# A hybrid decoder step: its first stage, channel tile by channel tile

## The chip, the cores and the metric

One core of one Trainium2 chip. The metric is the device time of one execution in microseconds (us); the kernel before takes 1694.86 us, the median of 3 runs (1690.61 to 1696.72). TensorE (PE) multiplies matrices, VectorE (DVE), ScalarE (ACT) and GpSimd (POOL) work element by element, and SyncE (SP) issues the DMA transfers.

## The reference

A prompt of 1024 tokens and a sample group of 8 x 4 = 32 tokens pass through two layers of width 1024: sliding-window attention, then gated DeltaNet. Every layer starts with a modulated norm and an input projection:

```python
def modulate(x, c, norm_g, w_mod, b_mod):
    shift, scale, gate = jnp.split(jax.nn.silu(c) @ w_mod + b_mod, 3, axis=-1)
    h = rms_norm(x, norm_g) * (1 + scale[:, None]) + shift[:, None]
    return h, gate[:, None]
...
    q, k, v, z = jnp.split(h @ w_in, [SWA_Q_W, SWA_Q_W + SWA_KV_W, SWA_Q_W + 2 * SWA_KV_W], axis=-1)
```

`c` is one row for the prompt and one for each of the 8 sample sequences, so nine rows in all. For a channel `d` and a token `t`, `h[t, d] = x[t, d] * rms[t] * Sc[d] + Sh[d]`, where `rms[t]` is 1 over the root of the mean square of the token's row, `Sc = norm_g * (1 + scale)` and `Sh = shift`.

## The kernel before, in words

All of it is float32. A projection takes its operands as a high and a low part (`hhi`, `hlo` for `h`; `wh`, `wl` for weights), each rounded so that PE can multiply it at full rate, and adds three products: high x high, low x high, high x low. The 1056 tokens stand in three groups of columns, 0 to 384, 384 to 768 and 768 to 1056; the 1024 channels are eight tiles of 128 partitions. One block of 128 output columns over all tokens and channels is therefore 8 x 3 x 3 = 72 matmuls.

The first stage makes `h` with channels on partitions and projects the first two blocks (keys of the first pair of heads, queries of the first group). Its steps:

- Loads, all issued by SP: nine tiles of rows of `x` (`xload`, eight of 128 rows and one of the 32 sample rows), the constants between the first and the second, then `w_mod` in two halves of eight tiles (`wmod_load`, 512 columns each of shift and scale), with the weights of the two blocks between them.
- `sq` (L625): ScalarE squares each row tile and sums it.
- `scale_x` (L631 to L639): DVE makes 1/rms of one to three row tiles by twelve small operations (`rsqrt`, L200 to L205) and multiplies the rows of `x` by it, ScalarE for three of the nine.
- `turn_x` (L650 to L659): PE transposes the scaled rows, eight squares of 128 x 128 for a tile, four to a bank of PSUM. ScalarE copies the first bank to `zo[0]`, DVE the second to `zo[1]`.
- `modulation_rows` (L311 to L322): silu of `c`, turned by PE into `cT`; the norm's weights and the bias, turned into `gT` and `bT`.
- `modulation` for one half of the channels: 16 matmuls (32 instructions, L344) into four strips of partitions, a copy `ma` by ScalarE (L354), and four matmuls with `fold64` (L360) that add the strips and turn them. `modulation_put` (L370 to L375) makes `Sh` and `Sc`.
- `shape_h(i)` for a half (L671 to L684): DVE (even tiles) or ScalarE (odd) makes `fu = zo * Sc + Sh` over the 1024 prompt columns, ScalarE rounds it to `hhi` (L674), DVE or GpSimd subtracts for `hlo` (L675). The 32 sample columns go by four GpSimd operations for four tiles together.
- `first_half(i, p_, kks)` (L702): the projection, half by half: first four channel tiles for the keys, the same four for the queries, then the other four for keys and for queries. The second half's modulation is interleaved by hand with the first tiles.

Around these steps a scheduler places the instructions of each engine; `issue_after` fixes some orders. Behind the stage come `kproj` and `qproj`, which empty the six banks (`khh`, `kll` at L823 to L826; `qs` at L889 and L890), the second query block (`project`, L567), the values (`vproj`, L1240) and then attention. From there on a planner (`Core`, whose wrapper is L89) writes down the order of each engine's instructions: it keeps a modelled time for every engine, counts each DMA at 0.45 us of issue and 2.4 us to landing, and lets pieces of work enter between projection matmuls when they are due. Weights of the projections are loaded by `load_raw` in pieces of 64 or 128 columns (L444), one projection ahead, and split by `split_w` (L456 on ScalarE, L457 on GpSimd). `keys_out` writes new keys and values, and copies the 124 kept rows of each sample cache from DRAM to DRAM.

Of the kernel before, what the change touches and what calls it, by code (L numbers as in the profile page):

```python
# [31 lines left out]
def constants():  # L32
# [35 lines left out]
    order = ["ident", "iu", "ones", "mku", "lo32", "bsel", "fold32", "fold64", "wmask", "hsel", "smask", "selp", "sels"]  # L68
# [151 lines left out]
def body(tc, I, O, cst_ap, dbg=None):  # L220
    nc = tc.nc
    from contextlib import ExitStack, nullcontext
    es = ExitStack()
# [29 lines left out]
    XB, FB, ZK, HK0, HK1 = 14, 3, 5, 7, 3  # L253
# [11 lines left out]
    gT = cp.tile([P, 2, KD], F32, name="gT")  # L265
    bT = cp.tile([P, 48], F32, name="bT")
# [9 lines left out]

    def xload(t):
        xt = xp.tile([P, D], F32, tag="xt", name="xt", bufs=XB)[0:P if t < NB else TS]
        nc.sync.dma_start(xt, xp_rows[t * P:(t + 1) * P] if t < NB else xs_rows)
        return xt  # L280

    def wmod_load(i):

        wms = []
        for k in range(KD):
            wt = xp.tile([P, D], F32, tag="xt", name="wm0", bufs=XB)
            nc.sync.dma_start(wt.rearrange("p (j c) -> p j c", j=2),
                              I["w_mod"][0, k * P:(k + 1) * P, 0:2 * D].rearrange("p (j c) -> p j c", j=2)[:, :, 512 * i:512 * i + 512])
            wms.append([wt[:, j * 512:(j + 1) * 512] for j in range(2)])
        return wms  # L290

    xts = [xload(0)]
    cst = cp.tile([P, nkeep], F32, name="cst")
    nc.sync.dma_start(cst, cst_ap[:, 0:nkeep])
    C = {k: cst[:, o:o + w] for k, (o, w) in COFF.items() if o < nkeep}
    ident = C["ident"]
    xts.append(xload(1))
    craw = xp.tile([P, D], F32, tag="fu", name="craw", bufs=FB)[0:9]
    nc.sync.dma_start(craw[0:1], I["c_prompt"])
    nc.sync.dma_start(craw[1:9], I["c_sample"])  # L300
    rows = xp.tile([64, P], F32, name="rows")
    nc.sync.dma_start(rows[0:16], I["norm_g"].rearrange("l (k p) -> (l k) p", p=P))
    nc.sync.dma_start(rows[16:64], I["b_mod"].rearrange("l (k p) -> (l k) p", p=P))
    xts += [xload(t) for t in range(2, NB + 1)]
    wm_half = [wmod_load(0)]

    x3 = None

    def modulation_rows():
        ce = xp.tile([P, D], F32, tag="fu", name="ce", bufs=FB)[0:9]  # L310
        nc.scalar.activation(ce, craw, AF.Tanh, scale=0.5)  # L311
        nc.gpsimd.tensor_scalar(ce, ce, 0.5, 0.5, ALU.mult, ALU.add)
        nc.gpsimd.tensor_tensor(ce, ce, craw, ALU.mult)
        nc.gpsimd.memset(cT, 0.0)
        pt = psb()
        for k in range(KD):
            nc.tensor.transpose(pt[:, k * 16:k * 16 + 9], ce[:, k * P:(k + 1) * P], ident[0:9, 0:9])
        nc.vector.tensor_copy(cT[:, :, 0:9], pt[:, 0:KD * 16].rearrange("p (k c) -> p k c", c=16)[:, :, 0:9])
        pt = psb()
        nc.tensor.transpose(pt[:, 0:64], rows, ident[0:64, 0:64])  # L320
        nc.vector.tensor_copy(gT.rearrange("p l k -> p (l k)"), pt[:, 0:16])
        nc.vector.tensor_copy(bT, pt[:, 16:64])  # L322

    Sh = [cp.tile([P, KD, 9], F32, name=f"Sh{l}") for l in range(2)]
# [3 lines left out]
    def modulation(l, load, js=(0, 1)):  # L328


        step, end = modulation_steps(l, load, js)
        for k in range(KD):
            step(k)
        return end

    def modulation_steps(l, load, js, pm=None):
        pm = pm or psb("mi")
        nj = len(js)

        def step(k):  # L340
            for q, wt in enumerate(load(k)):
                if nj == 1:
                    q += 2 * (k % 2)
                mm = nc.tensor.matmul(pm[32 * q:32 * q + 32, :], cT[:, k, :], wt,  # L344
                                      start=(k <= 2 - nj), stop=(k >= KD - 3 + nj), skip_group_check=True)
            return mm

        return step, lambda: modulation_end(l, js, pm)

    def modulation_end(l, js, pm):  # L350
        nj = len(js)
        w = 64 * nj
        ma = wp.tile([P, 512], F32, tag="wr", name="ma", bufs=4)
        nc.scalar.copy(ma, pm)  # L354
        mT = psb()
        for c in range(4):
            if nj == 2:
                mm = nc.tensor.transpose(mT[:, c * w:(c + 1) * w], ma[:, c * P:(c + 1) * P], ident)
            else:
                mm = nc.tensor.matmul(mT[:, c * w:(c + 1) * w], ma[:, c * P:(c + 1) * P], C["fold64"], start=True, stop=True)  # L360
        modulation_put(l, js, mT)
        return mm

    def modulation_put(l, js, mT):
        w = 64 * len(js)
        mv = mT[:, 0:4 * w].rearrange("p (c r) -> p c r", r=w)
        for q, j in enumerate(js):
            bs = bT[:, 24 * l + 4 * j:24 * l + 4 * j + 4]
# [254 lines left out]
    for t in range(NB + 1):  # L623
        parts = P if t < NB else TS
        sqs.append(nc.scalar.activation(sq[0:parts], xts[t], AF.Square, accum_out=xss[0:parts, t:t + 1]))  # L625
# [82 lines left out]
    for i, ts in enumerate(xb):  # L708
        last = nxt
        if i < 3:  # L710
            nxt = scale_x(xb[i + 1])
# [2014 lines left out]
```

## Time and profile before

| | us |
|---|---|
| median of 3 runs | 1694.86 |
| lowest, highest run | 1690.61, 1696.72 |
| span of the profiled execution | 1699.2 |
| PE busy in it | 1613.3 |
| DVE, ACT, POOL busy | 1207.9, 865.5, 581.8 |

The profile is of one execution, and its span, from the first to the last instruction, is the only time that it has; it is 4.3 us longer than the median of the runs. Times in it count from its first instruction. In a row of the timeline stand start, busy time, engine, line of the kernel, operation, what it writes and reads, shape, count, and in brackets how long the engine was idle before and what ended that. Rows merge neighbours of one kind: "x4" are four instructions. Matmul ends are modelled and overlap, so a pace is best read from one start to the next.

### The profile page before, as it was taken

The numbers are of one execution on the slowest core, as the hardware profiler recorded it, in microseconds if no ns is written. First come the engines' busy times: TensorE is split into PE (matmuls) and PEld (weight loads), VectorE is DVE, ScalarE is ACT, GpSimd is POOL, SyncE is SP. The second block draws the span as 40 slices with busy tenths as digits, with TensorE's granted clock in tenths as the row PEclk, the third lists the DMA queues.
The fourth block names the chain that finished last, engine by engine and source line by source line (L and its number), as shares of the span: only waits on it lengthen the run. The fifth ranks groups of instructions, "written<-read, shape, count | busy, mean of one in ns | idle before, by whom it ended". The sixth has DMA issues, their size and how long they took to land. (4 is left out here: it accounts for less than half of the span.)

```text
span 1699.2 us, 31431 instructions
## 1 busy us (share of the span) xinstructions
PE 1613.3 (95%) x10554; PEld 1417.4 (83%) x10554; DVE 1207.9 (71%) x3540; ACT 865.5 (51%) x2517; POOL 581.8 (34%) x1042
## 2 busy tenths in 40 slices
PE   6999999998999999999999999999999998989896
PEld 4988888986678899988989999899999996667784
DVE  5526676564665578878889788788788876367776
ACT  6625565443344565366463755655656654233332
POOL 2501111111222334363442644345344454333232
PEclk9999999998999999999999999999999999999998
DMA  9532121223343232132422324124241237855885
GB/s 345 158 123 73 53 59 48 59 81 93 116 136 105 79 77 65 59 99 73 118 56 69 89 66 129 46 79 111 54 124 49 55 97 225 245 165 169 243 259 166
DMA packets 281571, 191.76 MB, mean 113 GB/s; under 512 B 98361, under 2 KB 253881, under 8 KB 281378
## 3 DMA queue, kind: packets, MB, share of 16 engines
q1 hardware_dynamic: 281410, 189.75, 38.8%
q8 instruction: 84, 1.38, 0.4%
q14 instruction: 77, 0.63, 0.1%
HBM read 144.68 MB, written 47.04 MB: 113 GB/s over the span
## 5 line engine op out<-in xcount | busy, mean ns | idle before, releaser
L89 PE MATMUL ps_pj<-h2hi,wh 128*128 128x384 f32 (+1 forms) x1128 | 380.1, 337 | 0.0
L89 PE MATMUL ps_pj<-h2hi,wl 128*128 128x384 f32 (+1 forms) x1128 | 378.9, 336 | 0.6 <-POOL wl L89 0.5
L89 PE MATMUL ps_pj<-h2lo,wh 128*128 128x384 f32 (+1 forms) x1128 | 379.3, 336 | 0.0
L89 POOL TENSOR_TENSOR wl<-wr,wh 128x512 fp32r<-128x512 f32 x122 | 165.0, 1354 | 533.2 <-ACT wh L89 470.7
L89 PEld LDWEIGHTS ps_pj<-h2hi,wl 128*128 128x128 f32 x1128 | 213.5, 189 | 4.6 <-POOL wl L89 1.2
L89 PEld LDWEIGHTS ps_pj<-h2hi,wh 128*128 128x128 f32 x1128 | 213.5, 189 | 2.4
L89 PEld LDWEIGHTS ps_pj<-h2lo,wh 128*128 128x128 f32 x1128 | 213.2, 189 | 2.6
L89 POOL TENSOR_TENSOR xt<-xt,y 128x512 f32<-128x512 f32 (+1 forms) x48 | 63.6, 1329 | 174.3 <-DVE y L89 140.7
L89 PE MATMUL ps_pj<-hlo,wh 128*128 128x384 f32 (+1 forms) x360 | 119.6, 332 | 0.0
L89 PE MATMUL ps_pj<-hhi,wh 128*128 128x384 f32 (+1 forms) x360 | 119.0, 331 | 0.0
L89 PE MATMUL ps_pj<-hhi,wl 128*128 128x384 f32 (+1 forms) x360 | 118.7, 330 | 0.0
L89 DVE SCALAR_TENSOR_TENSOR vT<-XR,cT,vT 128x384 f32<-128x384 f32 (+1 forms) x144 | 91.8, 644 | 21.8 <-ACT vT L89 20.3
L89 DVE TENSOR_TENSOR X<-X,tmp 64x31 f32<-64x31 f32 (+15 forms) x248 | 94.5, 381 | 8.5
L89 DVE TENSOR_TENSOR tmp<-X 64x31 f32<-64x31 f32 (+15 forms) x248 | 95.9, 387 | 4.8 <-POOL X L89 1.5
L89 ACT CAST wh<-wr 128x512 fp32r<-128x512 f32 x122 | 75.1, 616 | 15.3 <-PE ps_pj L89 11.9
L89 PEld LDWEIGHTS ps_pj<-hlo,wh 128*128 128x128 f32 x360 | 68.2, 189 | 11.2 <-issue 11.1
L89 ACT COPY XR<-ps_pj 128x384 f32<-128x384 f32 (+1 forms) x96 | 43.2, 450 | 64.7 <-PE ps_pj L89 64.6
L89 PEld LDWEIGHTS ps_pj<-hhi,wh 128*128 128x128 f32 x360 | 68.3, 190 | 2.7 <-issue 2.7
L89 PEld LDWEIGHTS ps_pj<-hhi,wl 128*128 128x128 f32 x360 | 68.2, 189 | 2.1 <-issue 2.1
L89 ACT ACTIVATE prob<-prob,nm 128x256 f32<-128x256 f32 (+1 forms) x128 | 62.2, 489 | 14.9 <-DVE nm L89 14.7
L89 POOL TENSOR_TENSOR Xd<-Xc,cst 32x128 f32<-32x128 f32 x128 | 63.6, 497 | 16.1 <-DVE UZ L89 6.7
L89 ACT ACTIVATE qe<-ps_mi,Eg 128x128 f32<-128x128 f32 x112 | 35.0, 364 | 65.6 <-PE ps_mi L89 65.6
(575 smaller groups left out, 4177.2 us busy)
## 6 DMA issues: line engine op xcount, KB each, us to landing
wr<-in_gdn_w_in SPq DMA_DIRECT2D x96, 256.0 KB
S<-in_state_gdn_s SPq DMA_DIRECT2D x40, 256.0 KB
xt<-in_x_prompt SPq DMA_DIRECT2D x16, 512.0 KB
wm<-in_w_mod SPq DMA_DIRECT2D x16, 512.0 KB
wr<-in_swa_w_in SPq DMA_DIRECT2D x64, 128.0 KB
wmod<-in_w_mod SPq DMA_DIRECT2D x32, 256.0 KB
wm<-in_w_mod SPq DMA_DIRECT2D x32, 256.0 KB
DP<-gcr SPq DMA_DIRECT2D x64, 128.0 KB
```

Of the source, the lines that this page charges most:

```text
L89: inst = fn(*args, **kwargs)
```

## The change

The stage is written anew, channel tile by channel tile, and the planner's wrapper now stands around it, so that each compute engine follows the order of the program:

- The host lays out the inputs in other order (no arithmetic): `w_mod`'s shift and scale columns in eighths (`wm0`, one channel tile each, two loads of 512 KB with 4 KB for a partition), the nine rows of `c` with channels on partitions and norm weights and bias already turned (`cgb`), `swa_w_in` in blocks of 128 output columns (`winb`), the first two blocks' weights for two channel tiles at a time (`win01`), the values' weights (`winv`).
- SP's loads of the stage are held in one order (`queued`): x first, with only `ident` and `fold32` of the constants, then two eighths with the first weights, the other constants, and so on.
- Rows of `x` are turned as they are. DVE copies both banks of a tile. 1/rms is made in two parts, of five row tiles and of four, and spread over all partitions by nine small matmuls (`spread_x`) into `rsb`.
- For each channel tile: `modulate` (8 matmuls of 256 columns), `fold` (2 matmuls with `fold32`, two DVE operations for `Sc` and `Sh`), `shape_h` (DVE: `u = zo * Sc * rsb`; ScalarE: `hhi = u + Sh`; DVE: `hlo = u + Sh - hhi`; four small GpSimd operations for the sample columns), then both blocks' projections.
- In `keys_out`, the two cache copies are issued only after the write of the new values.

The core of the diff:

```diff
+    queue = []
+    def queued(dst, src):
+        inst = nc.sync.dma_start(dst, src).ins
+        if queue:
+            tc.add_manual_dep(inst, queue[-1], ...)
+        queue.append(inst.name)
...
+    def turn_x(n, t):
+        parts = P if t < NB else TS
+        for kk in range(2):
+            pt = psb(("pj3", "lg", "pj3", "lg", "pj3", "ob")[(2 * n + kk) % 6])
+            for j in range(4):
+                k = kk * 4 + j
+                nc.tensor.transpose(pt[:, j * parts:(j + 1) * parts], xts[t][:, k * P:(k + 1) * P],
+                                    ident[0:parts, 0:parts])
+            nc.vector.tensor_copy(zo[kk][:, :, t * P:t * P + parts],
+                                  pt[:, 0:4 * parts].rearrange("p (q t) -> p q t", q=4))
+        nc.scalar.activation(sq[0:parts], xts[t], AF.Square, accum_out=xss[0:parts, n:n + 1])
+
+    def scale_x(n0, n1):
+        sv = sm.tile([P, n1 - n0], F32, tag="sv4", name="sv4")
+        nc.vector.tensor_scalar(sv, xss[:, n0:n1], 1.0 / D, EPS, ALU.mult, ALU.add)
+        rsqrt(nc, sm, rsx[:, n0:n1], sv, n1 - n0, tag=f"rx{n0}")
+
+    def spread_x(gi):
+        a, b = GRP[gi]
+        pb = psb(("lg", "ob", "lg")[gi])
+        for t in range(3 * gi, 3 * gi + 3):
+            parts, n = P if t < NB else TS, turns_x.index(t)
+            nc.tensor.matmul(pb[:, t * P - a:t * P - a + parts], rsx[0:parts, n:n + 1].to_broadcast([parts, P]),
+                             ident[0:parts, 0:parts], start=True, stop=True)
+        nc.scalar.copy(rsb[:, a:b], pb[:, 0:b - a])
...
+    def modulate(e):
+        pm = psb("mi")[:, 0:256]
+        for k in range(KD):
+            q = k % 4
+            nc.tensor.matmul(pm[32 * q:32 * q + 32, :], cT[:, k, :], wms[e, k // 4][:, q, :], start=(k < 4), stop=(k >= 4),
+                             skip_group_check=True)
+        ma = xp.tile([P, 256], F32, tag="ma", name="ma", bufs=2)
+        nc.scalar.copy(ma, pm)
+        return ma
+
+    def fold(e, ma):
+        mT = psb("mi")
+        for c in range(2):
+            nc.tensor.matmul(mT[:, 32 * c:32 * c + 32], ma[:, c * P:(c + 1) * P], C["fold32"], start=True, stop=True)
+        nc.vector.tensor_scalar(Sc[0][:, e, :], mT[:, 32:41], bS[:, e:e + 1], gT[:, 0, e:e + 1], ALU.add, ALU.mult)
+        nc.vector.tensor_scalar(Sh[0][:, e, :], mT[:, 0:9], bT[:, e:e + 1], None, ALU.add)
+
+    def shape_h(k):
+        u = xp.tile([P, TP], F32, tag="fu", name="fu", bufs=FB)
+        sc, sh = Sc[0][:, k, 0:1], Sh[0][:, k, 0:1]
+        spans = [slice(0, GW), slice(GW, TP)]
+        for cs in spans:
+            nc.vector.scalar_tensor_tensor(u[:, cs], zo[k // 4][:, k % 4, cs], sc, rsb[:, cs], ALU.mult, ALU.mult)
+            nc.scalar.activation(hhi[:, k, cs], u[:, cs], AF.Identity, bias=sh)
+        for cs in spans:
+            nc.vector.scalar_tensor_tensor(hlo[:, k, cs], u[:, cs], sh, f(hhi[:, k, cs]), ALU.add, ALU.subtract)
...
+    def first_part(k, p_):
+        hi, lo = fws[k // 2]
+        for gi, (a, b) in enumerate(GRP):
+            for n, (x, y) in enumerate(((hi, hhi), (hi, hlo), (lo, hhi))):
+                nc.tensor.matmul(fps[p_][gi], x[:, 2 * p_ + k % 2, :], y[:, k, a:b], start=(k == 0 and n == 0),
+                                 stop=(k == KD - 1 and n == 2))
+
+    wmod_load(0)
+    first_load(0)
+    wmod_load(1)
+    for n, t in enumerate(turns_x):
+        turn_x(n, t)
+        if n == 1:
+            modulation_rows()
+        if n == 4:
+            scale_x(0, 5)
+    queued(cst[:, early:], cst_ap[:, early:nkeep])
+    wmod_load(2)
+    first_load(1)
+    spread_x(0)
+    scale_x(5, 9)
+    ma = modulate(0)
+    fws[0] = split_w(fraws.pop(0))
+    spread_x(1)
+    spread_x(2)
+    fold(0, ma)
+    shape_h(0)
+    ma = modulate(1)
+    wmod_load(3)
+    for k in range(KD):
+        if k + 1 < KD:
+            fold(k + 1, ma)
+            shape_h(k + 1)
+        first_part(k, 0)
+        if k % 2 == 0 and k + 2 < KD:
+            fws[k // 2 + 1] = split_w(fraws.pop(k // 2 + 1))
+        first_part(k, 1)
+        if k + 2 < KD:
+            ma = modulate(k + 2)
+        if k + 4 < KD:
+            wmod_load(k + 4)
+            if k % 2 == 0:
+                first_load(k // 2 + 2)
...
                 for new, old in ((nks, "cache_swa_k"), (nvs, "cache_swa_v")):
-                    nc.sync.dma_start(new[:, 0:P - DS, :], I[old][0].rearrange("b s h d -> b s (h d)")[:, DS:P, :])
+                    with tc.issue_after(values.ins):
+                        nc.sync.dma_start(new[:, 0:P - DS, :], I[old][0].rearrange("b s h d -> b s (h d)")[:, DS:P, :])
...
-        plan = [(win, {"k": lambda b: [(0, 1024 + b * P, P)], "q": lambda b: qpieces(b // 4, b % 4), "z": zpieces}[a](b))
-                for a, b in ORDER]
+        plan = [(winb[{"k": 0, "q": 2, "z": 10}[a] + b], [(0, 0, P)]) for a, b in ORDER]
```

The row tiles are turned in the order 0, 1, sample rows, 2 to 7 (`turns_x`).

285 lines of the change are left out of this document (88 added, 197 removed).

## The prediction

> **What bounds the kernel now.** I read the page first, then the stages in time, then the first 68 us engine by engine. The page:
>
> ```profile
> span 1699.2 us, 31431 instructions
> PE 1613.3 (95%) x10554; PEld 1417.4 (83%) x10554; DVE 1207.9 (71%) x3540; ACT 865.5 (51%) x2517; POOL 581.8 (34%) x1042
> ```
>
> TensorE (PE) is busy for 95% of the span. The table of stages says where it is not:
>
> ```profile
> 0.00:67.00 67.00, 50.40 (x304) 39.75 (x305) 38.29 (x92) 41.09 (x63) 28.76 (x28) 1.00 0.79 261
> 67.00:110.00 43.00, 42.40 (x322) 38.95 (x320) 9.98 (x27) 14.80 (x43) 7.62 (x6) 1.00 0.51 154
> ```
>
> After the name of a stage and its length stand the busy times of PE, weight loads, VectorE (DVE), ScalarE (ACT) and GpSimd (POOL), then the clock, the DMA share and GB/s. The first 67 us, which are all that the change rewrites, have 16.6 us of idle PE; the 43 us behind them have 0.6. Whatever the first stage saves or loses therefore passes on to a PE that is full. In order of time on PE:
>
> ```profile
> 16.14 1.11 PE L650 MATMUL ps_pj<-cst,xt 128*128 128x128 f32 x4 [3.96 <-DVE xt L639]
> 23.84 1.06 PE L650 MATMUL ps_pj<-cst,xt 128*128 128x128 f32 x4
> 24.69 1.06 PE L650 MATMUL ps_lg<-cst,xt 128*128 128x128 f32 x4
> ...
> 32.40 2.78 PE L344 MATMUL ps_mi<-wm,cT 128*32 128x512 f32 x24
> 35.95 1.10 PE L360 MATMUL ps_mi<-cst,ma 128*128 128x64 f32 x8 [0.76 <-ACT ma L354]
> 36.98 2.77 PE L344 MATMUL ps_mi<-wm,cT 128*32 128x512 f32 x20
> 39.68 0.44 PE L702 MATMUL ps_pj<-hhi,wh 128*128 128x384 f32 x1
> ...
> 49.82 0.33 PE L702 MATMUL ps_lg<-hhi,wh 128*128 128x384 f32 x1
> ...
> 55.63 0.33 PE L702 MATMUL ps_pj<-hhi,wh 128*128 128x384 f32 x1
> ...
> 67.26 0.33 PE L567 MATMUL ps_pj<-hhi,wh 128*128 128x384 f32 x1
> ```
>
> The transposes wait for rows that DVE has to scale first; the modulation waits for its weights; the projection (L702) starts at 39.7 and has ended at 67.26, where the next projection (L567) starts. From 49.82 to 55.63 it does four channel tiles for one block of weights: 5.81/4 = 1.45 us, so a channel tile for both blocks is 2.9 us and all eight are 23.2. The remaining 4.3 of the 27.6 us are the rest of the second modulation, its fold and short waits.
>
> **The change, part by part.** The new stage is a chain up to the first projection matmul, S, and then a loop up to the end E. I work out both and compare E with 67.26.
>
> *Loads.* Their amount is the same, their order is x first, then w_mod in eighths. ScalarE and the DMA view (GB/s in 40 slices of the first 60 us) give the arrivals:
>
> ```profile
> 4.61 1.28 ACT L625 ACT_TABLE_LOAD   x1 [4.61 <-DMA xt<-in_x_prompt]
> 7.31 1.06 ACT L625 ACTIVATE sq<-xt 128x1024 f32<-128x1024 f32 x1 [0.25 <-DMA xt<-in_x_prompt]
> GB/s 0 145 400 380 310 412 412 407 415 300 276 388 388 385 386 388 386 341 264 359 388 382 378 384 385 387 308 166 322 91 379 24 105 149 0 0 0 0 0 0
> ```
>
> x0 lands at 4.6. Between it and x1 come 836 KB now and 592 KB then, so x1 lands at 6.5; at some 386 GB/s each further 512 KB takes 1.36 us, the small pieces 0.5: x7 at 15.2, w_mod's first eighth (1 MB) at 17.9, the second, behind weights, at 21.3, the last at about 40. The loop below wants the last one at about 54, so the loads bound nothing; the new layout as such is costed at nothing, with 14 us of cover.
>
> *Rows and 1/rms.* Each row tile is eight transposes. Their pitch is 24.69 - 23.84 = 0.85 for four, 1.7 for a tile, slower than it arrives. They start at about 5.1 (ident), the 32 sample rows take 0.8, and x7 is through at 5.1 + 8 x 1.7 + 0.8 = 19.5. All copies out of PSUM now fall to DVE (ScalarE did half), with two chains for 1/rms between them:
>
> ```profile
> 7.09 0.15 DVE L631 TENSOR_SCALAR sv<-xss 128x1 f32<-128x1 f32 x1 [7.09 <-ACT sq L625]
> 9.40 0.75 DVE L639 TENSOR_SCALAR xt<-xt,rs 128x1024 f32<-128x1024 f32 x1
> ...
> 26.89 1.28 DVE L659 COPY zo<-ps_lg 128x512 f32<-128x512 f32 x2
> ```
>
> A chain is 9.40 - 7.09 = 2.3 us, a copy 0.6. Program order puts the first chain behind the fifth tile: 13.5 + 2.3 = 15.8, then four tiles at 1.2 reach 20.6, and the second chain 22.9. The scaling of the rows goes (0.75 or 1.15 a tile), and with it PE's waits; late next is this second chain. 1/rms is then spread over partitions by nine small matmuls, two instructions each at the transposes' 0.21: six of the nine follow the chain, 2.2 us cold, 1.1 at full clock. The squares, tanh, and the shorter modulation rows run beside arrivals; without that cover they would cost their 1.2 us a tile on ScalarE.
>
> *To the first matmul.* Needed are rows for fold, ScalarE's copy, shaping and GpSimd:
>
> ```profile
> 35.31 0.58 ACT L354 COPY ma<-ps_mi 128x512 f32<-128x512 f32 x1 [1.75 <-PE ps_mi L344]
> 37.65 1.24 ACT L673 ACTIVATE fu<-zo,Sh,Sc 128x1024 f32<-128x1024 f32 x1 [1.76 <-DVE Sc L375]
> 83.35 0.37 ACT L1245 COPY vsb<-ps_pj 128x256 f32<-128x256 f32 x1 [0.50 <-PE ps_pj L1240]
> 37.09 0.20 DVE L370 TENSOR_TENSOR Sh<-ps_mi,bT 128x36 f32<-128x36 f32 x1 [4.29 <-PE ps_mi L360]
> 39.59 1.54 DVE L675 TENSOR_TENSOR hlo<-fu,hhi 128x512 fp32r<-128x512 f32 x2
> 41.85 2.61 DVE L675 TENSOR_TENSOR hlo<-fu,hhi 128x1024 fp32r<-128x1024 f32 x1 [0.72 <-ACT hhi L674]
> L89 DVE SCALAR_TENSOR_TENSOR zo<-th,zo 128x384 f32<-128x384 f32 x16 | 9.1, 570 | 0.6
> 40.95 2.44 POOL L675 TENSOR_TENSOR hlo<-fu,hhi 128x1024 fp32r<-128x1024 f32 x1 [0.96 <-ACT hhi L674]
> L89 POOL TENSOR_TENSOR us<-us,tp 128x32 f32<-128x32 f32 x96 | 30.2, 314 | 8.0
> ```
>
> A fold is now four instructions, half of L360's eight: 0.5. Two DVE operations, 0.5 with the handover. The new three-operand product is not in the trace with 640 columns: at least 0.57 (its 384), at most 1.6 (2.61 x 640/1024, beside GpSimd); I take 0.85, nearest to 0.77 for 512. So 1.4 for both halves, 0.95 for ScalarE on the second half. Behind that on ScalarE's queue stands the copy of the next eighth, 0.37 + 0.1, and PE's fold of that eighth (0.5) is queued ahead of the first projection matmul. Sum: 0.5 + 0.5 + 1.4 + 0.95 + 0.5 + 0.5 = 4.4. S = 22.9 + 2.2 + 4.4 = 29.5, or 28.4 at full clock; I take 29.3. That is 10.4 us earlier than 39.7.
>
> *The loop.* What stood ahead of the projection now stands inside it. Per channel tile PE does 2.9 us of projection, then modulates an eighth, waits for ScalarE, folds. An eighth is 16 instructions of 256 columns; 24 of 512 took 2.78, so 0.058 each, 0.93, with the tail 1.03 (bounds 0.85, and 1.86 if a short one cost as much as a long one). The wait was 0.76 with a copy of 0.58; with 0.37 it is 0.56, and nothing covers it, since PE's order holds the projection behind the fold. So 1.03 + 0.56 + 0.5 = 2.1 us, six times after S: 12.5. E = 29.3 + 23.2 + 12.5 = 65.0.
>
> DVE per tile has 0.4 + 2 x (0.57 + 0.85) = 3.2 us; from the end of one fold to the last hlo it is 3.8 with ScalarE between, against a period of 5.0 plus 0.5 until that hlo is read. GpSimd's four small sample operations (0.3 to 0.8 each) and every second tile a weight split slow it: the 1024 column subtraction took 2.61, not twice 0.77, beside GpSimd's 2.44. I add 0.5 us over the loop (0 to 7).
>
> *Hand-over.* Before, the keys' banks were complete at 61.4 (55.63 + 5.8), 5.8 us ahead of the queries' last matmul; now both end together. The first key bank is complete 2.4 us before E, but the next projection needs it empty:
>
> ```profile
> 63.55 0.54 DVE L825 TENSOR_TENSOR kll<-ps_pj,khh 64x384 fp32r<-64x384 f32 x1
> 64.11 0.55 DVE L826 TENSOR_TENSOR kll<-ps_pj,khh 64x384 fp32r<-64x384 f32 x1
> 62.08 0.47 ACT L823 CAST khh<-ps_pj 64x384 fp32r<-64x384 f32 x1
> ```
>
> 0.57 for the first cast and four subtractions at 0.57 are 2.9 us: PE waits 0.5, with handovers 0.7. The next banks follow behind 4.2 us of matmuls each. Later projections only load in larger pieces; SP issues half as many, and PE waited for no weights there: 0.
>
> *Moved copies.* Two 992 KB cache copies leave SP's queue at 40.4 and 86.5 us for behind the values, some 20 us later than the second; next weights and modulation weights queue behind them:
>
> ```profile
> 40.44 0.86 SPq L89 DMA_DIRECT2D out_new_k_s<-in_cache_swa_k  x1
> 86.52 0.74 SPq L89 DMA_DIRECT2D out_new_v_s<-in_cache_swa_v  x1
> 110.00:200.00 90.00, 87.77 (x598) 74.71 (x596) 57.26 (x223) 51.90 (x177) 11.86 (x9) 1.00 0.29 84
> ```
>
> 1.6 us of issue, 2.6 us of transfer each at 386 GB/s, in a stage where DMA is 29% busy and weights are asked for one projection (12.6 us) ahead: 0, at most 5.
>
> **Sum.** 65.0 + 0.5 + 0.7 = 66.2 against 67.26: 1.1 us less, 1698.1 on the profiled execution's 1699.2. The median of the runs is 1694.86, 4.3 below that span, so 1693.8. A start 10 us earlier is nearly all given back inside the loop.
>
> **Rivals.**
>
> *A. The projection begins at half clock.* This clock exists here:
>
> ```profile
> 411.00:414.00 3.00, 0.98 (x24) 0.88 (x24) 1.98 (x10) 1.14 (x2) 0.00 (x0) 0.86 0.18 49
> 414.00:417.00 3.00, 2.44 (x3) 1.17 (x4) 0.09 (x1) 0.36 (x1) 0.00 (x0) 0.50 0.69 224
> 417.00:420.00 3.00, 3.00 (x7) 1.85 (x6) 0.52 (x1) 1.88 (x5) 0.00 (x0) 0.50 0.03 5
> 26.54 1.49 PE L344 MATMUL ps_mi<-wm,cT 128*32 128x512 f32 x2
> 30.61 0.60 PE L650 MATMUL ps_lg<-cst,xt 128*128 128x128 f32 x4
> ```
>
> After a thin stretch the granted clock was 0.50, and dense work needed some 5.3 us (414.6 to 419.9) to get it back. The transposes too took 1.06 for four before 26.5 us and 0.60 at 30.6, though the clock column shows 1.00 there. In the old stage modulations stood between transposes and projection; in the new one PE has only spreads, two eighths and two folds in the last 10 us before S, with idle gaps of up to 2.3. If S falls into half clock, 5.3 us do 2.65 us of work: 1693.8 + 2.7 = 1696.5. The Trainium skill, "TensorE: Matmul & The Clock Gate", section "Part 4: PE-mode transpose", says that transposes do not count as busy for the clock; by that rule the rows of transposes warm nothing, and this rival would be likely. Our trace agrees so far: the transposes ahead of 26.5 stayed at their long pace, and quicker ones are seen 4 us after the first modulation matmul. Against it: spreads and eighths are real matmuls, on PE for 6 to 8 of the 10 us before S, a longer run than those 4. 20%.
>
> *B. VectorE sets the loop (slower).* If GpSimd's operations meet DVE's in every tile, 2 x 1024 columns at 2.61 are 5.2, with folds and handover 6.2 us. It decides from 5.5 on. 0.7 us a tile over eight tiles (the first delays S), and 1 more at the hand-over: 1693.8 + 6.6 = 1700.4, slower than before. For it: the 2.61 row. Against: GpSimd has 1.6 us of sample work a tile, and 1.3 for a split every second, not 5. 17%.
>
> *C. All terms at their low ends.* Warm from the spreads on (S 28.4), 0.93 + 0.5 + 0.42 in the loop (11.1), hand-over hidden: E = 62.7, 4.6 less: 1690.3. 16%.
>
> *D. The planned stages shift.* The planner counts every DMA that is issued, and half of the weights' DMAs are gone; an order that comes out otherwise, or the moved copies, could move the waits of those stages. Price up to 8 us, either way: 1686 or 1702. 9%.
>
> *E. The change's order isn't reached*, since loads wait: at half the rate the last eighth lands at 65, 11 us late, which gives 1705; 14 us of slack speak against it; 2%.
>
> **Numbers.** Forecast 36%, the rest as given; its own range is 1691 to 1696. A to C and most of D lie between 1686 and 1702, which with 3 us between runs of one kernel is the range. Within 0.5% (8.5 us, about what a measurement of this kernel can tell from no change) lie the forecast and nearly all of A, B and C. Faster by more than that: D's lucky half and the low edge of C, 10%; slower: B's far end, D and E, 12%; within: 78%.
>
> **What would show it.** First L702-like matmul at 28 to 31, not 39.7; transposes still at 0.85 for four; DVE's second chain ending near 23; PE waiting some 0.56 for "ma" in each of six tiles and nothing like that for hlo; one wait below 1 us after the last first-stage matmul; the next projection at 65 to 67. An hlo wait in each tile would show B, clock below 1 around 30 us A. Wrong would be the whole sum if the transposes keep up with the arrivals (S by 3 us earlier), or if PE's idle time after 110 us changes by several us.

## The result, and the profile after

The changed kernel takes 1704.05 us (median of 6 runs, 1702.11 to 1707.83) against 1694.51 us (6 runs, 1690.61 to 1698.17) of the kernel before on the same chip: a ratio of 1.0055, 95% interval 1.0037 to 1.0073, or 9.5 us more. It is slower, just beyond the 0.5% that a measurement can tell from no change; the forecast was 1.1 us faster. Chips and executions differ by several us here: the execution of before that the prediction read, with its span of 1699.2, took longer than any of these six runs, and on other chips the median of before was 1699.5 to 1701.2. So ratios below are always against before on the same chip.

The page of the changed kernel, its first lines, and its two stages:

```profile
span 1700.9 us, 31581 instructions
PE 1620.1 (95%) x10643; PEld 1428.9 (84%) x10643; DVE 1214.1 (71%) x3546; ACT 859.2 (51%) x2516; POOL 581.8 (34%) x1065
```

```profile
0.00:67.00 67.00, 53.41 (x377) 44.83 (x378) 40.72 (x90) 29.63 (x52) 24.03 (x49) 0.92 0.60 230
67.00:110.00 43.00, 40.30 (x283) 36.79 (x282) 13.35 (x27) 19.08 (x51) 10.36 (x8) 0.92 0.50 167
```

The first row gained 3 us of busy PE and still isn't done at 67; the second, which had 0.6 us of idle PE, now has 2.7, and both have a granted clock of 0.92. PE's timeline says where:

```profile
14.46 0.60 PE L89 MATMUL ps_pj<-cst,xt 128*128 128x128 f32 x4
24.23 0.93 PE L89 MATMUL ps_ob<-cst,rsx 128*128 128x128 f32 x4 [2.80 <-DVE rsx L89]
30.72 1.06 PE L89 MATMUL ps_mi<-cst,ma 128*128 128x32 f32 x4 [1.29 <-ACT ma L89]
31.59 0.67 PE L89 MATMUL ps_pj<-hhi,wh 128*128 128x384 f32 x1
37.74 0.63 PE L89 MATMUL ps_mi<-cst,ma 128*128 128x32 f32 x4 [0.55 <-ACT ma L89]
42.92 0.63 PE L89 MATMUL ps_mi<-cst,ma 128*128 128x32 f32 x4 [0.55 <-ACT ma L89]
...
73.03 0.66 PE L542 MATMUL ps_pj<-hhi,wh 128*128 128x384 f32 x1 [2.66 <-DVE kll L803]
```

The spreads wait 2.80 us for the second 1/rms; the first projection matmul, S, stands at 31.59; from one fold to the next a tile takes 7.02 us the first time (30.72 to 37.74) and 5.18 after that; the next projection (L542) starts at 73.03, after a wait of 2.66 for the keys' bank, where L567 started at 67.26. The clock by stage (PEclk is the third number from the end of a row):

```profile
24.00:26.00 2.00, 1.77 (x9) 1.55 (x9) 0.16 (x1) 0.48 (x1) 0.00 (x0) 0.64 1.04 416
26.00:34.00 8.00, 6.71 (x35) 5.24 (x35) 5.48 (x11) 3.05 (x6) 4.32 (x10) 0.50 1.03 407
34.00:36.00 2.00, 2.00 (x12) 1.96 (x10) 1.05 (x2) 1.01 (x2) 1.19 (x2) 0.80 1.02 397
36.00:68.00 32.00, 28.68 (x235) 23.49 (x234) 19.39 (x36) 12.99 (x23) 15.26 (x28) 1.00 0.17 61
68.00:73.00 5.00, 2.37 (x14) 2.13 (x15) 3.57 (x8) 4.84 (x11) 2.25 (x2) 0.94 0.52 158
73.00:80.00 7.00, 6.97 (x24) 7.00 (x25) 5.36 (x11) 5.45 (x14) 5.00 (x4) 0.56 0.94 336
```

Both pauses, 2.80 and 2.66 us, are followed by half clock, once for about 10 us and once for 7. In the second stretch PE is full, so (1 - 0.56) x 7 = 3.1 us are lost outright. That is this execution; in the second trace of the same program (e5) half clock behind the hand-over ends after 3.4 us, and 1.6 are lost.

To place all versions on one scale I use one instruction that occurs once, far behind the first stage: ScalarE's copy of the second key pair's last columns. In before and after:

```profile
237.76 0.29 ACT L89 COPY kx<-ps_pj 128x160 f32<-128x160 f32 x1 [1.00 <-DVE kll L89]
```

```profile
243.28 0.29 ACT L89 COPY kx<-ps_pj 128x160 f32<-128x160 f32 x1 [1.00 <-DVE kll L89]
```

### The profile page after: what moved, and what is told of

Its sections match the earlier page's. It is cut to its first block, busy times and chain, and to the rows that moved or that the text cites. A ratio compares the mean times of both kernels' runs of the same rounds, so it can differ in the third digit from the quotient of the medians.

```text
span 1700.9 us, 31581 instructions
## 1 busy us (share of the span) xinstructions
PE 1620.1 (95%) x10643; PEld 1428.9 (84%) x10643; DVE 1214.1 (71%) x3546; ACT 859.2 (51%) x2516; POOL 581.8 (34%) x1065
## 5 line engine op out<-in xcount | busy, mean ns | idle before, releaser
L89 POOL TENSOR_TENSOR wl<-wr,wh 128x512 fp32r<-128x512 f32 x128 | 175.9, 1376 | 546.1 <-ACT wh L89 469.4
L89 PE MATMUL ps_pj<-hlo,wh 128*128 128x384 f32 (+1 forms) x376 | 125.0, 332 | 0.0
L89 PE MATMUL ps_pj<-hhi,wh 128*128 128x384 f32 (+1 forms) x376 | 124.7, 332 | 0.0
L89 PE MATMUL ps_pj<-hhi,wl 128*128 128x384 f32 (+1 forms) x376 | 123.8, 329 | 0.0
L89 ACT CAST wh<-wr 128x512 fp32r<-128x512 f32 x128 | 78.6, 616 | 15.2 <-PE ps_pj L89 12.3
L89 PEld LDWEIGHTS ps_pj<-hlo,wh 128*128 128x128 f32 x376 | 71.0, 189 | 11.5 <-issue 11.1
```

What stands on the lines that cost most here:

```text
L89: inst = fn(*args, **kwargs)
```

## The experiments

Theory 1: the loss is made in the first stage and at its hand-over (half clock around S, PE's wait for the keys' bank, half clock behind that). Theory 2: the later weights in blocks, the moved cache copies or the planner's order cost it. Rivals to single points stand with the runs. All versions, by next projection, marker (as above) and ratio to before on the same chip:

| run | next projection | marker | ratio, 95% interval |
|---|---|---|---|
| before; again (e9) | 67.26; 65.99 | 237.76; 236.56 | 1; 0.9997 (0.9979 to 1.0014) |
| after; again (e5) | 73.03; 73.82 | 243.28; 242.72 | 1.0055 (1.0037 to 1.0073); 1.0039 (1.0022 to 1.0056) |
| e1, e13 later only | 67.90; 66.81 | 236.27; 236.72 | 1.0016 (1.0001 to 1.0032); 1.0006 (0.9991 to 1.0020) |
| e11 copies only | 69.60 | 237.98 | 1.0006 (0.9986 to 1.0025) |
| e10, e14 first only | 75.53; 73.32 | 246.17; 243.97 | 1.0069 (1.0048 to 1.0090); 1.0052 (1.0035 to 1.0070) |
| e2 keys last | 70.69 | 244.00 | 1.0045 (1.0028 to 1.0062) |
| e3 idle matmuls | 71.42 | 240.40 | 1.0042 (1.0025 to 1.0059) |
| e4 lag 2 | 75.16 | 244.14 | 1.0043 (1.0027 to 1.0059) |
| e6 bank order | 72.97 | 242.21 | 1.0037 (1.0020 to 1.0054) |
| e7 lag 1 and bank order | 72.75 | 240.61 | 1.0028 (1.0013 to 1.0043) |
| e12 copy hidden | 70.47 | 239.44 | 1.0031 (1.0018 to 1.0044) |
| e8 all repairs | 67.76 | 235.61 | 1.0009 (0.9992 to 1.0026) |
| e15 order | 69.09 | 239.20 | 1.0012 (0.9998 to 1.0026) |
| e16 order, no idle matmuls | 66.82 | 236.24 | 0.9998 (0.9985 to 1.0011) |
| e17 banks | 63.36 | 232.86 | 0.9968 (0.9953 to 0.9983) |

An interval is some 5 us wide, so single ratios tell the ends of the table apart and not its neighbours; the traces tell the rest. They have a scatter of their own. Up to the end of VectorE's second chain for 1/rms the programs after, e4 to e7, e10, e12 and e14 do the same work, and yet that chain ends between 23.00 us (e6) and 25.63 (e10): with the landing of x's second row tile, for which PE waits up to 1.56 us (e10), and with the moment at which the transposes come to full pace (between 8.5 us in e6 and 16.2 in e12). This moves next projection and marker alike.

**Which part of the change: e1, e13, e11, e10, e14, e9, e5.** In the first two only the later parts are put into before:

```diff
-        plan = [(win, {"k": lambda b: [(0, 1024 + b * P, P)], "q": lambda b: qpieces(b // 4, b % 4), "z": zpieces}[a](b))
-                for a, b in ORDER]
+        plan = [(winb[{"k": 0, "q": 2, "z": 10}[a] + b], [(0, 0, P)]) for a, b in ORDER]
...
-                    nc.sync.dma_start(new[:, 0:P - DS, :], I[old][0].rearrange("b s h d -> b s (h d)")[:, DS:P, :])
+                    with tc.issue_after(values.ins):
+                        nc.sync.dma_start(new[:, 0:P - DS, :], I[old][0].rearrange("b s h d -> b s (h d)")[:, DS:P, :])
```

e11 has the second edit alone; e10 and e14 undo both in the changed kernel; e9 and e5 are before and after themselves, once more.

> The kernel before, with its whole first stage kept; only the weights of the later projections come in blocks and the two cache copies are moved behind the values. Theory 1 (the loss is made in the first stage and at its hand-over): ratio 1.000 to the kernel before, within 0.0015, and the planned stages stand where they stood. Theory 2 (the later weights, the moved copies or the planner's order cost the part that the first 75 us do not show, some 4 us): ratio 1.0025.

> The kernel of the first experiment once more (before, with the later weights in blocks and the copies moved). If blocks or copies cost 2 to 3 us: ratio 1.0016 again, and both together exclude 1.000. If that was chance: ratio 1.000 within 0.0015.

> The kernel before with only the two cache copies moved behind the values; weights as they were. Theory 1: ratio 1.000 within 0.0015. Theory 2 (the copies, now in the queue ahead of the second projection's weights, delay a load that PE waits for): ratio 1.0015, with a wait of PE between 90 and 130 us that the kernel before hasn't.

> The changed kernel with its first stage, but the later projections' weights taken from the old array in pieces and the two cache copies issued where they were: the complement of the first experiment. Theory 1 (all of the loss is made in the first 75 us): ratio as the changed kernel's, 1.0045 within 0.0015, next projection at 73 us. Theory 2 (the blocks and the moved copies cost 2 to 3 us of it): ratio 1.003.

> The kernel with only the new first stage once more. Its first trace had the next projection at 75.5 us, 2.5 later than the changed kernel's, with the same instructions in the first stage. If that was the execution's own scatter in the time at which the transposes come to full clock: next projection at 73 to 74.5, ratio 1.0045 to 1.006. If the pieces of the later weights cost it: 75.5 again, ratio 1.007.

> The kernel before itself once more, as a measure of what two executions of one program differ by. Ratio 1.000 within 0.002. In its trace the next projection starts between 66 and 67.3 us (the one shown starts at 67.26); how far the instructions of the planned stages stand from those of the first trace shows which differences of the other traces can be noise: expected up to 3 us either way behind 375 us, below 1 us between 130 and 375.

> The changed kernel itself once more, to have it on the chip of the three below and to see how far its traces agree. Ratio to the kernel before 1.0055 within 0.002; the first matmul of the next projection at 73 us within 0.5, with a wait of 2.7 us ahead of it.

The first stage alone (e10, e14) is as slow as the whole change, and the later parts alone stand at the marker where before stands (236.27 to 237.98, before 236.56 and 237.76). Theory 1 holds for where the loss is. In e14 the next projection came at 73.32, so e10's 75.53 was scatter: its second chain ended 2.3 us later (25.63 and 23.31). e5's next projection, at 73.82, missed what I had expected of it by 0.3 us. The later parts aren't without effect, though. In e11, ScalarE and PE at the hand-over:

```profile
63.51 0.62 ACT L456 CAST wvh<-wr 128x512 fp32r<-128x512 f32 x1 [2.99 <-DMA wr<-in_swa_w_in]
64.04 0.61 ACT L456 CAST wh<-wr 128x512 fp32r<-128x512 f32 x1
64.56 0.47 ACT L824 CAST khh<-ps_pj 64x384 fp32r<-64x384 f32 x1
```

```profile
69.60 0.41 PE L567 MATMUL ps_pj<-hhi,wh 128*128 128x384 f32 x1 [2.23 <-DVE kll L827]
```

With the copies out of its way the split of the values' weights comes ahead of the keys' evacuation on ScalarE, waits there for its load, and PE waits 2.23 us for the keys' bank (2.13 in e1, 2.00 in e13). Most of it comes back before the marker: before has 1.4 us of idle PE between 104 and 116 us, e11 none.

```profile
104.00:116.00 12.00, 10.59 (x78) 8.33 (x76) 3.67 (x20) 3.22 (x13) 1.29 (x1) 1.00 0.44 122
```

```profile
104.00:116.00 12.00, 12.00 (x96) 10.58 (x95) 3.16 (x17) 3.33 (x11) 0.17 (x1) 1.00 0.40 139
```

I had expected such a wait behind 90 us, or none. Theory 2 keeps this much: the interval of e1 alone excludes 1, that of e13 doesn't, and the two don't exclude a cost of up to 3 us. The order of VectorE, ScalarE and GpSimd behind 130 us is the same in the traces of before and after but for six neighbouring VectorE operations near 360 us.

**The hand-over: e2, e4, e6, e7.** e2 is before with one exchange:

```diff
-    first_half(1, 0, range(4))
-    first_half(1, 1, range(4))
+    first_half(1, 1, range(4))
+    first_half(1, 0, range(4))
```

> The kernel before, with one pair of lines exchanged: the last four channel tiles of the queries are multiplied ahead of those of the keys, so that the keys' banks are complete only at the end of the first stage, as they are in the changed kernel. Theory 1 (a late first key bank stalls the next projection and the pause brings half clock): PE waits 2 to 3 us at the hand-over, the granted clock falls to 0.5 for some 5 us behind it, and the time is 4 to 6 us above the kernel before (ratio 1.0025 to 1.0035). Rival, as the prediction had it: a wait below 1 us, clock unchanged, ratio 1.0005.

```profile
70.69 0.66 PE L567 MATMUL ps_pj<-hhi,wh 128*128 128x384 f32 x1 [4.20 <-DVE kll L826]
71.15 0.52 PE L567 MATMUL ps_pj<-hlo,wh 128*128 128x384 f32 x1
```

```profile
71.00:78.00 7.00, 7.00 (x26) 7.00 (x26) 5.30 (x12) 5.78 (x17) 5.00 (x4) 0.59 0.34 86
```

That late keys alone, with nothing else of the change, cost 4.20 us of wait and then 0.41 x 7 = 2.9 us of half clock, 6 to 7 us at the marker. That is more than I had expected, because the bank takes longer to empty. The reason in the changed kernel, on ScalarE and VectorE:

```profile
67.99 0.47 ACT L800 CAST khh<-ps_pj 64x384 fp32r<-64x384 f32 x1
...
70.75 0.47 ACT L800 CAST khh<-ps_pj 64x384 fp32r<-64x384 f32 x1
71.24 0.47 ACT L801 CAST khh<-ps_pj 64x384 fp32r<-64x384 f32 x1
...
71.75 0.56 DVE L802 TENSOR_TENSOR kll<-ps_pj,khh 64x384 fp32r<-64x384 f32 x1 [0.18 <-ACT khh L801]
72.32 0.56 DVE L803 TENSOR_TENSOR kll<-ps_pj,khh 64x384 fp32r<-64x384 f32 x1
```

The first bank holds two heads. ScalarE casts the first head of all three banks and only then (70.75) the second head of the first; A head's first subtraction waits for both of its casts (71.75 behind 71.71), and VectorE has two subtractions of the second bank in between. Its last one ends at 72.88, 4.9 us after the first cast. Before took the same time, 62.08 to 66.97, beside 5.8 us of queries.

Two edits were to mend it: the queries two tiles behind the keys (e4), and the banks evacuated one after the other (e6).

```diff
+        if k >= LAG:
+            first_part(k - LAG, 1)
...
-                    with tc.issue_after(last_split[0].ins):
-                        evac(gi, a, b, fps[0][gi])
+                    with tc.issue_after(prev.ins):
+                        prev = evac(gi, a, b, fps[0][gi])
```

> The changed kernel, with the queries' channel tiles two tiles behind the keys', so that the keys' first bank is complete 5.3 us before the stage ends. The amount of work is the same. Theory 1 (hand-over wait 2.7 us and the half clock behind it 2.65 us): both go, the time is 4.5 to 5.5 us below the changed kernel, ratio to the kernel before 1.0025. Theory 2 (the rest lies in later stages): the hand-over's wait goes, 2.7 us, but the planned projections still stand 4 us late, ratio 1.004.

> The changed kernel, with the evacuation of the keys' banks in order of the banks: both heads of the first bank, then the second, then the third (in the changed kernel the first head goes through all its banks on ScalarE first, and the first bank is empty with the sixth subtraction). Theory 1: the first bank is empty at 71.3 in place of 72.9, PE's wait is 1.1 in place of 2.7 us; if the granted clock then stays at 1.00, 2.6 us more are saved: 1.6 to 4.2 us below the changed kernel. Rival (the end of the shaping sets the wait, not the order of the evacuation): wait 2.7 us as before, same time.

> The changed kernel with the evacuation in order of the banks, and the queries' channel tiles one tile behind the keys', so that the keys' banks are complete 3.9 us before the stage ends and no weight split waits for a lagging tile. Theory 1: the first bank is empty 3.5 us after it is complete, so PE's wait is below 0.5 us, no half clock follows, and the next projections stand 5 us earlier than in the changed kernel (some 1 us later than in the kernel before): ratio to the kernel before 1.0025. Theory 2 (the planned stages give it back): the hand-over's wait goes, but the time stays within 2 us of the changed kernel.

e4 and e6 failed as repairs. In e4 the keys were early, but on ScalarE the split of the next weights, which stands ahead of the casts, waited for a buffer that the lagging query tiles still read, and VectorE for the sinks, which are loaded late:

```profile
69.10 0.62 ACT L89 CAST wh<-wr 128x512 fp32r<-128x512 f32 x1 [1.14 <-PE ps_ob L89]
...
70.43 1.25 DVE L758 TENSOR_SCALAR nsk<-sk 128x8 f32<-128x8 f32 x2 [3.77 <-DMA wr<-in_winv]
```

PE waited 3.08 us (75.16). The ratio is near theory 2's number, but not for its reason, since the wait didn't go. In e6 VectorE followed the new order, but ScalarE's casts of the second head stayed where they were (70.70), and so did the wait, 2.66: it tells nothing of the order's worth. In e7 ScalarE kept its order too (second head at 70.48) and the bank again takes 4.9 us (67.72 to 72.61), so its gain is the lag's alone: PE waits 1.23 us, 1.43 less, which is one tile of queries (1.45). That is more than the 0.5 expected, and the clock stays at 1.00; the marker is 2.4 us ahead of the mean of the two traces of after (243.0), the ratio 1.0028. What the order is worth shows only in e17 below, where it is written out beside the same lag. ScalarE there:

```profile
58.89 0.47 ACT L834 CAST khh<-ps_pj 64x384 fp32r<-64x384 f32 x1
...
61.08 0.47 ACT L834 CAST khh<-ps_pj 64x384 fp32r<-64x384 f32 x1
```

The second head's casts follow the first's, with 1.14 us of the values' weights between them; the bank is empty after 4.3 us (63.21), and PE waits 0.66.

**Around S, and the loop: e3, e12, e8.** 

```diff
     fws[0] = split_w(fraws.pop(0))
+    idle_pe(20)
     spread_x(1)
...
     ma = modulate(1)
+    idle_pe(8)
```

> The changed kernel, with 20 matmuls of ident by ident on PE between the second spread's wait and its start, and 8 behind the second eighth's modulation; they feed nothing. Theory 1 (the pause of 2.8 us ahead of the spreads drops the clock, and S then comes at half clock): granted clock 1.00 from 24 to 36 us, S near 30 in place of 31.6, and the first tile at full pace: first stage 3 to 4 us shorter, ratio to the kernel before 1.0035. Rival (VectorE's chain to the first hlo sets S, whatever PE's clock): S stays within 0.5 us and the time falls by 1.5 us at most, ratio 1.0047.

```profile
24.00:36.00 12.00, 11.37 (x102) 9.57 (x101) 7.27 (x17) 4.82 (x9) 5.75 (x11) 1.00 1.03 405
```

```profile
30.97 0.63 PE L89 MATMUL ps_mi<-cst,ma 128*128 128x32 f32 x4 [0.22 <-ACT ma L89]
31.44 0.42 PE L89 MATMUL ps_pj<-hhi,wh 128*128 128x384 f32 x1
```

The clock is 1.00 from 24 to 36 us and the first tile takes 5.17 us (to 36.14) in place of 7.02. From the start of the spreads to the fold behind the first tile after takes 13.51 us (24.23 to 37.74) and e3 10.54 (25.60 to 36.14), so half clock cost 3.0 us, 1.85 of them in the first tile. S is at 31.44, hardly earlier than 31.59, as the rival had it, but not for its reason: the spreads start 1.4 us later, half of it since the second chain ended later in this execution (24.84, not 24.17), half since the 20 matmuls ran until 25.8. The next projection comes 1.6 us earlier and the marker 2.6 (mean of after); the ratio alone wouldn't show it.

e12 moves the modulation, so that ScalarE copies beside the queries' part:

```diff
-        first_part(k, 1)
         if k + 2 < KD:
             ma = modulate(k + 2)
+        first_part(k, 1)
```

> The changed kernel, with each eighth's modulation between the keys' and the queries' part of a tile, so that the copy to ma lies beside 1.45 us of matmuls. Theory 1 (the loop is PE's own work plus a wait of 0.55 for ma in each of six tiles): period 4.6 in place of 5.15, stage 3.3 us shorter, ratio lower than the changed kernel's by 0.002. Rival (VectorE's chain per tile sets the loop as soon as PE gets faster): period 5.0 or above, with waits for hhi or hlo in each tile, ratio lower by less than 0.001.

```profile
38.45 0.53 PE L89 MATMUL ps_mi<-cst,ma 128*128 128x32 f32 x4
42.98 0.53 PE L89 MATMUL ps_mi<-cst,ma 128*128 128x32 f32 x4
```

The tile takes 4.53 us with no wait for `ma`, `hhi` or `hlo` but 0.2 us for `hlo` in the last tile (65.33; the changed kernel has the same at 67.89): PE's own work sets the loop, and VectorE keeps up at that pace too. The marker is 3.6 us earlier.

> The changed kernel with all repairs: evacuation in order of the banks, queries one tile behind, 20 and 8 idle matmuls that keep PE busy ahead of S, and each eighth's modulation put between the keys' and the queries' part, so that ScalarE's copy (0.55 us a tile, six times) lies beside matmuls. Theory 1, with all three losses additive: 5.3 + 2.9 + 3.3 = 11.5 us below the changed kernel, 2 us below the kernel before, ratio 0.999. Rival (VectorE's chain, 3.8 us a tile, now sets the loop): 3 us more, ratio 1.0005 or above, with waits for hlo in the loop.

Alone e3, e12 and e7 gained 2.6, 3.6 and 2.4 us at the marker, 8.6 in all; together 7.4: the marker at 235.61 is 1.5 us ahead of before's mean (237.2), the ratio 1.0009, and there is no wait for hlo but 0.2 us in the last tile. Counted from the end of the second chain, so without the scatter ahead of it, the gains are 2.9, 4.4 and 3.2 us, and 8.1 together. The 11.5 I expected counted the hand-over at its full 5.3, of which a wait of 1.22 us stayed here.

**A version that beats both: e15, e16, e17.** The pause of 2.80 us ahead of the spreads has a cause of its own, on VectorE and GpSimd of the changed kernel:

```profile
20.80 0.16 DVE L89 TENSOR_SCALAR sv<-xss 128x4 f32<-128x4 f32 x1
...
21.60 1.20 DVE L89 SCALAR_TENSOR_TENSOR rst<-rst,sv 128x4 f32<-128x4 f32 x1
...
24.01 0.16 DVE L89 SCALAR_TENSOR_TENSOR rsx<-rst,rsw 128x4 f32<-128x4 f32 x1
```

```profile
21.52 1.26 POOL L89 TENSOR_TENSOR wl<-wr,wh 128x512 fp32r<-128x512 f32 x1 [12.20 <-ACT wh L89]
```

All copies stand ahead of the second chain, and one operation of four columns takes 1.20 us beside GpSimd's weight split: it ends with it, at 22.80 and 22.78. In e15 and e17, where the split comes behind the chain, the same operation takes 0.16. e15 and e16 put the chain ahead of the last two rows' copies, and more:

```diff
     for n, t in enumerate(turns_x):
         turn_x(n, t)
         if n == 4:
             scale_x(0, 5)
+        if n == 6:
+            scale_x(5, 9)
...
+        if k == 0:
+            ma2 = modulate(2)
         first_part(k, 0)
```

> The changed kernel with another order of the same work: squares issued ahead, the second chain for 1/rms before the copies of the last two rows of x, the weight split behind it, the third eighth ahead of the first tile, later eighths between the keys' and the queries' part, queries one tile behind, keys evacuated bank by bank with the order written out, the sinks loaded early; and 6 + 4 idle matmuls in the gaps ahead of S. Theory 1 (every wait found lies on the path): S at 27 to 28.5 us, tile period 4.1 to 4.6, next projection at 61.5 to 63 without a wait, 4 to 5 us ahead of the kernel before, ratio 0.997 within 0.001. Rival (VectorE, with 12 us of copies and two chains until 24, then sets S in any order): S at 30 or later, next projection at 65 or later, ratio 0.9995 or above.

> As the one before, without the idle matmuls. If pauses of about 2 us ahead of S drop the clock: granted clock near 0.5 for some 5 us around S and the next projection 2 to 3 us later than with them, ratio higher by 0.0015. If the shorter pauses don't: clock 1.00, the same times.

S came at 35.42 and 32.28, as the rival had it, but not for its reason:

```profile
24.52 1.65 PE L89 MATMUL ps_ob<-cst,rsx 128*128 128x128 f32 x6 [3.32 <-DVE zo L89]
```

The chain was done at 22.07 in e15; of the 3.32 us that PE waited, 2.45 came after that, for a PSUM bank that the copies moved behind the chain still read. e16 has the same 2.45 (19.12 to 21.57):

```profile
21.57 1.45 PE L89 MATMUL ps_ob<-cst,rsx 128*128 128x128 f32 x6 [2.42 <-DVE zo L89]
```

A wait was removed and a bank put in its place. The granted clock fell in both (0.66 and 0.50 from 26 to 32 us), and the pair says nothing against the idle matmuls: e15's S is 3.1 us later, but its chain ended 2.95 later already, and from the chain's end to the marker both take 217.1 us. They were worth nothing here, where I had expected 2 to 3 us if the clock dropped without them. e17 changes the bank, and puts the split ahead of the second spread:

```diff
-        pb = psb(("lg", "ob", "lg")[gi])
+        pb = psb("mi")
```

> As e16 (no idle matmuls), with the three spreads in PSUM banks that the rows' copies don't use and the first weight split ahead of the second spread. Theory 1 (the wait for a bank was what held S and dropped the clock): the second spread starts at 22 us, no pause of PE above 1.2 us between 18 us and S, granted clock 1.00, S at 27 to 28.5, next projection at 61.5 to 63.5: 3 to 4.5 us ahead of the kernel before, ratio 0.998 within 0.0013. Rival (VectorE's copies and chains set S in any order): S at 29.5 or later, next projection at 65 or later, ratio 0.9995 or above.

```profile
21.89 1.49 PE L89 MATMUL ps_mi<-cst,rsx 128*128 128x128 f32 x10 [0.70 <-DVE rsx L89]
27.15 0.63 PE L89 MATMUL ps_mi<-cst,ma 128*128 128x32 f32 x4 [2.21 <-ACT ma L89]
29.32 0.69 PE L89 MATMUL ps_pj<-hhi,wh 128*128 128x384 f32 x1
31.82 0.53 PE L89 MATMUL ps_mi<-cst,ma 128*128 128x32 f32 x4
36.36 0.53 PE L89 MATMUL ps_mi<-cst,ma 128*128 128x32 f32 x4
...
63.36 0.41 PE L542 MATMUL ps_pj<-hhi,wh 128*128 128x384 f32 x1 [0.66 <-DVE kll L837]
```

The next projection starts at 63.36, within what was expected; S at 29.32 is 0.8 later than the latest expected, and the pause of 2.21 us for ScalarE's copy to `ma` is longer than the 1.2 I had allowed; it brings half clock at S (0.72 from 26 to 32). From the chain's end to S it takes 7.48 us, where e16 took 13.16. The ratio is 0.9968 (0.9953 to 0.9983): 5.4 us faster than before, measured once, in 12 runs on one chip, and faster than after. So the change's idea pays once the waits that it brought with it are gone.

## Why the prediction was wrong

The forecast for the next projection was 66.2 and 73.03 was measured, 6.8 us later. By the prediction's own steps:

- **Loads**: right in this trace, where nothing in the stage waits long for a transfer; in others PE waits for x's second row tile, 1.56 us in e10.
- **Transposes**: wrong with little effect. They went at 0.85 for four only until 14.3 us, then at 0.44, and ended at 18.0 in place of 19.5; VectorE's copies, forecast to end at 20.6, started the second chain at 20.80.
- **Second chain**: its end was to be 22.9 and was 24.17, mostly for the one operation of 1.20 us beside GpSimd. I had moved the weight split at no cost. 1.3 us.
- **S**: 7.4 us behind the chain's end in place of 6.4, at half clock; so S came at 31.59, not 29.3. Here **rival A** happened, to which I gave 20%. Its price was about right in this trace: 1.0 us ahead of S and 1.5 from S through the first tile (6.62 in place of 5.16), 2.5 against the 2.7 that I had written. In e6, e10 and e14, with the same stage, it was 3.5 to 3.6, since half clock lasted longer. Its cause was in my own sum: I had a pause of PE of up to 2.3 us there and took the spreads and eighths for work enough. The half clock that I quoted from before, at 414 us, begins in a pause of 2.58 us, which the prediction didn't weigh:

```profile
414.56 3.75 PE L89 MATMUL ps_lg<-modG,selt 128*128 128x512 f32 x4 [2.58 <-issue]
```

- **The loop**: 5.16 a tile in the mean in place of 5.0, and 0.55 us of wait for `ma` (0.56 forecast) in each. Over the five tiles behind the first this is 0.8 us; the last two took 0.5 us more than forecast, 0.2 of it a wait for `hlo`. **Rival B** is refuted by e12.
- **Hand-over**: with what follows it, the step that failed by most. I had the bank empty after one cast and four subtractions, 2.9 us, and a wait of 0.7; it takes 4.9 us, since both casts of a head come ahead of its subtractions and the second head's casts stand behind the first head's three banks, and PE waits 2.66. The trace of before held this (62.08 to 66.97), hidden by 5.8 us of queries. 2.0 us, and the 3.1 us of half clock behind it (1.6 in e5) were in no case of mine.

2.3 for S, 3.0 in the loop (1.6 in the first tile, 0.8, 0.5 and 0.1 of rounding) and 2.0 at the hand-over are 7.3 in all, against 0.5 that I had added for VectorE: 6.8.

- **Behind the stage**: forecast 0, and from the next projection to the marker it is: 170.50 us in before, 170.25 in after. But 3.1 us lost to half clock are hidden in it, and so something was given back: 2.1 us by the later parts if they do here what they do in e1 and e11 (168.4 from next projection to marker); where the rest comes from isn't traced. **Rival D**'s shift of the planned stages didn't happen, nor did E's wait for loads; of **rival C**'s low ends none came.

At the marker after is 5.8 us late (mean of two traces against mean of two), while its times say 6.8 and 9.5, with intervals of about 3 us on either side. Several other versions also took 1 to 4 us more than their marker says, e1 and e10 alike, e16 and e17 hardly. The traces show no further loss: from the marker to the end the two of before take 1461.4 and 1456.5 us, the two of after 1457.6 and 1462.8. But the scatter there is wide. All versions lie between 1456.5 and 1472.5, the two traces of before, matched instruction by instruction, are 1.2 us apart at the marker and up to 6.8 behind 400 us, which is more than I had expected, and much of this goes with half clock in the later stages: e15, with 1457.5, has a granted clock of 0.987 there, e8, with 1472.5, 0.980. So whether the rest of the measured loss is more than scatter stays open.

## What to carry to other kernels

Before a stage is reordered, list for each bank and buffer at its end how long it takes to empty and what covers that now; a cover that goes costs the wait, and behind waits of 2.66 us and more it cost another 1.6 to 3.1 us of half clock here. A chain of small operations on the critical path must not share its time with another engine's long one, nor its PSUM banks with copies that come after it. An earlier start was worth nothing here until the waits between it and the full engine were gone, so trace the whole way to the next stage.

## What the runs showed of the hardware

Pauses of PE of 2.66 us and more brought the granted clock to 0.50 each time they stood ahead of the next projection (after, e2 to e6, e10, e12, e14), 0.6 to 1.23 us didn't (e7, e8, e15 to e17), and 2.0 to 2.2 us did so in some executions (e13, e17) and not in others (e1, e11). In the clock's record of every trace half clock stands in stretches of 3.41 us or two to four times that, unless the trace's end cuts one off. At the hand-over it was 6.83 in after and e2 and 3.41 in the eight others that have it there, which is why equal waits cost a full PE 1.6 to 1.7 us or 3.0 to 3.1. The Trainium skill, "TensorE: Matmul & The Clock Gate", section "Part 1: The HAM clock gate (the "warmup" mystery)", ties the drop to an idle window of about 3.4 us that runs freely; here pauses shorter than that were enough, and that equal pauses end differently fits a window that runs freely.

The Trainium skill, "TensorE: Matmul & The Clock Gate", section "Part 4: PE-mode transpose", says that transposes don't count as busy for the clock. The runs speak against it, for the transposes of this kernel (float32, 128 x 128; the trace doesn't name their mode). In the changed kernel PE ran nothing else from 4.83 to 18 us, and they came to full pace at 14.46, as its first row in the profile after shows. The clock's record agrees: its first entry, full clock, is at 14.34. The clock column shows 1.00 for 4.8 to 14 us as well, because time ahead of the first entry counts as full. In e1, e9 and e13, with the old first stage, the first entry (19.1 to 19.8 us) also comes behind transposes alone. In the trace that the prediction read it is at 27.46, 0.9 us behind the first modulation matmul and after some 10 us mostly of transposes, so that trace decided nothing, though the prediction took it as agreeing.
